# Weight-stationary products with both parts of the activations in one 512-column matmul, and the halves added in evacuation

## The chip, the cores and the metric

One NeuronCore of a Trainium2 chip runs the kernel. The metric is the device time of one execution in microseconds (us), as a median over runs; lower is better.

## The reference

Two blocks work on 256 tokens of width 1024, all in float32. Block one: a mixer (a stick-breaking attention and a gated recurrence `hgrn2_chunk_scan` side by side, merged by sigmoid gates), then a mixture of 16 experts with two experts per token. Block two: half a feed-forward, a mixer of 16 attention heads (banded, compressed and selected), half a feed-forward. Cut to the lines that make the products in question:

```python
def mixer_sublayer(...):                      # first mixer
    h = rmsnorm(x, ln1_g)
    proj = h @ w_in                           # q, k, v | q, f, i, g | two gates
    ...
    merged = (jax.nn.sigmoid(gate_sb) * (y_sb @ w_branch_sb)
              + jax.nn.sigmoid(gate_hg) * (y_hg @ w_branch_hg))
    return x + merged @ w_out

def swiglu(h, w_in, w_out):                   # the feed-forwards, D_FF = 2816
    gate, up = jnp.split(h @ w_in, 2, axis=-1)
    return (jax.nn.silu(gate) * up) @ w_out
```

## The kernel before, in words

**Two parts.** The weights come from DRAM as 1 MB units (`Stream`, tiles `raw`). Outside of the experts, `split_next` cuts each unit into two parts of a narrower float type (fp32r): ACT copies it to `whi` (L353) and DVE subtracts to get `wlo` (L365). The activations x^T are cut the same way into `hTh` and `hTl` (names in the code: `xh`, `xl`), each [128, 8, 256]: 8 blocks k of 128 inputs by 256 tokens. A product is the sum hi·xh + hi·xl + lo·xh. `unit` asks for the next unit's split before the present unit is multiplied, so the splits run one unit ahead in the in-order queues of ACT and DVE. The pool of 1 MB tiles (`big`) has six slots: the two parts of x^T and two pairs `whi`, `wlo`.

**The weight-stationary form.** `form_a` (L395) takes a [1024, 256] unit (or, for the branch products, [512, 512]) as the stationary operand. For each 128 columns c of it there are three groups of eight or four matmuls of 256 columns of tokens into one half of a PSUM bank `psa`:

```python
for k in range(kt):
    nc.tensor.matmul(ps[:, c % 2], hi[:, k, cs], xh[:, k, :], ...)   # L414
    nc.tensor.matmul(ps[:, c % 2], hi[:, k, cs], xl[:, k, :], ...)   # L415
for k in range(kt):
    nc.tensor.matmul(ps[:, c % 2], lo[:, k, cs], xh[:, k, :], ...)   # L419
```

After two such column blocks `evac` empties the bank. The evacuations are: `scaled` (L691, DVE, times the rows' scale `rb`) for the forget gate `sgf`, the query `qh`, the key `kT` and the two merge gates `gr`; `ev_sq` (L705) for `qT`; `ev_sb` and `ev_hg` for the branch products; and `ev` (L1434) in the feed-forward. The other forms are `form_b` and `out_unit` (L483, L490), where the weights are the moving operand, 512 columns at a time.

**What sets the order.** The first mixer (0 to 212 us) is written as one program with two side streams, the recurrence `hgrn` and the attention `stick`, which are interleaved with the units by an estimate of TensorE's clock (`tick`). Outside of the parts under `manual_schedule` the framework's scheduler puts the instructions of each engine into their order. Then come the experts (to 463 us), the first feed-forward (FFN1, to 655 us), the second mixer (to 784 us), which a list scheduler of the kernel (`Plan`) orders from written costs, and the second feed-forward (FFN2, to 970 us). The feed-forwards run in program order: two "q" units (one bank of 128 columns of gate and of up each) to one "o" unit (`out_unit`), a step later. `ev` of a q unit scales at once; its silu (L318), the product with the up half (L1438) and the split into `ah` (L386) and `al` (L387) are put off behind the next unit's split. At the end of FFN1 `then` adds to x (L1470) and makes y (L1474), `turn` transposes y (L1363), and the last split of that stage runs on POOL.

PSUM has four banks for these products in the first mixer, the experts and FFN1 (tag "d", four more have tag "s"). In the second mixer and FFN2 all eight have one tag; FFN2's sums hold five.

Of the kernel before, what the change touches and what calls it, by code (L numbers as in the profile page):

```python
# [10 lines left out]
F32 = mybir.dt.float32  # L11
# [30 lines left out]
RAW = (U_MIX + 6, U_MIX + 7)   # used as they are  # L42
# [17 lines left out]

def bcast_rows(ap2d, off, n):
# [3 lines left out]
def _order():  # L65
    """unit of each place in the stream: an expert's last two units follow the next one's first four"""
# [6 lines left out]
def _part(raw, k, n, c):  # L73
    """columns of block k of n, in a unit of one or more tiles"""
# [4 lines left out]
class Stream:  # L79
    """The packed weights, 1 MB units in the order of use, through slots in SBUF."""  # L80
# [8 lines left out]
    def add(self, pool, tag, bufs, end=N_UNITS, n=1, parts=1, between=None):  # L89
        """n slots, each of `parts` tiles, in a pool that lives until unit `end` is first needed"""  # L90
# [38 lines left out]
# when the parts of x^T are there, from the start of the second mixer  # L129
# [4 lines left out]
class Plan:  # L134
    """Instructions with what they read and write, put into an order by a list schedule:
    at each engine's next free moment the ready one with the longest way to go."""
# [7 lines left out]
    def hold(self, slot, n, key):  # L144
        """key keeps n of a slot's tiles from the start"""
# [3 lines left out]
    def op(self, eng, ns, fn, r=(), w=(), a=(), get=(), at=0.0, p=0.0, seq=None):  # L149
        """reads r, writes w, adds to a in any order; seq: a sequence to keep to"""  # L150
# [34 lines left out]
    def turn(self, key):  # L185
        """whether an addition to key is the first one, and the last one"""
# [9 lines left out]
    def order(self):  # L196
        """by the longest way to go, with a head start for some parts"""
# [71 lines left out]
class K:  # L269
# [6 lines left out]
    # ---- interleaving of instruction streams by an estimate of the PE's clock  # L276
# [26 lines left out]
    # ---- activation tables, in an order that loads each set once per phase  # L303
# [80 lines left out]

    def split(self, hi, lo, src):
# [3 lines left out]
    # ---- products  # L389
    def form_a(self, n, xs, evac, more=True, kt=8, cols=256, first=False):  # L390
        """[kt*128, cols] units as the stationary operand: out^T per 128 columns."""
        nc = self.nc
        xh, xl = xs
        for u in range(n):
# [3 lines left out]
            if first:  # L398
                ps = self.ps.tile([128, 2, 256], F32, name="psa", tag=self.tag("d"))
                for i, (w, v) in enumerate(((hi, xh), (hi, xl), (lo, xh))):  # L400
                    for k0 in (0, 4):
                        for c in range(2):
                            for k in range(k0, k0 + 4):
                                nc.tensor.matmul(ps[:, c], w[:, k, c * 128:c * 128 + 128], v[:, k, :], start=i + c + k == 0,  # L404
                                                 stop=i == 2 and k == kt - 1, skip_group_check=True)
                self.tick(48 * 109)
                evac(u, ps)
                continue
            for c in range(cols // 128):
# [3 lines left out]
                for k in range(kt):  # L413
                    nc.tensor.matmul(ps[:, c % 2], hi[:, k, cs], xh[:, k, :], start=k == 0, stop=False)  # L414
                    nc.tensor.matmul(ps[:, c % 2], hi[:, k, cs], xl[:, k, :], start=False, stop=False)  # L415
                    if k % 4 == 3:
                        self.tick(870)
                for k in range(kt):
                    nc.tensor.matmul(ps[:, c % 2], lo[:, k, cs], xh[:, k, :], start=False, stop=k == kt - 1)  # L419
# [4 lines left out]
    def form_b(self, xs, evac, ps=None):  # L424
        """two [512, n] units as the moving operand: out rows of tokens; with ps, the first one is done"""
# [1644 lines left out]
T4 = 16  # L2070
# [143 lines left out]
```

## Time and profile before

| | us |
|---|---|
| three runs | 974.76, 975.59, 978.01 |
| median | 975.59 |
| span of the profiled execution, first to last instruction | 973.7 |
| TensorE busy in it | 955.5 |
| VectorE (DVE) busy | 539.5 |
| ScalarE (ACT) busy | 408.1 |
| GpSimd (POOL) busy | 106.6 |

The profiled execution has no time of its own beside its span; the median lies 1.9 us above the span. The profile counts an engine as busy while it executes, PE stands for TensorE's matmuls, and PEclk is the clock that TensorE was granted, as a share of full speed. A matmul's own duration overlaps with the next one's, so the pitch of a row of matmuls (from start to start) is read from the chain of work that ended last or from the gaps between starts, not from the duration of one.

### The profile page before, as it was taken

Reading aid. Unit: us, or ns where it says so; the run is one execution under the profiler, and the core shown is the slowest. Engines: PE = TensorE matmul, PEld = TensorE weight load, DVE = VectorE, ACT = ScalarE, POOL = GpSimd, SP = SyncE. Lnnn points to the kernel's source line nnn. Section 1 sums busy time; section 2 is a strip of 40 time slices with the busy share of each in tenths; the row PEclk is TensorE's granted clock in tenths of the full one; section 3 lists DMA queues with packets and bytes.
Section 4 is the critical chain, followed back from the end, with each engine's and each line's share of the span. In section 5 each row is a group of like instructions: output and inputs, shape, how many; then the busy total and the mean of one; then the engine's idle time right before and its main releaser. Section 6 shows DMA issues by size and latency. Waiting matters only on the chain.

```text
span 973.7 us, 15302 instructions
## 1 busy us (share of the span) xinstructions
PE 955.5 (98%) x6320; PEld 762.2 (78%) x6320; DVE 539.5 (55%) x848; ACT 408.1 (42%) x635; POOL 106.6 (11%) x114
## 2 busy tenths in 40 slices
PE   7999999999999999999899999998999999999998
PEld 5997789997444344443799999997987799999997
DVE  5589937665212121222775655657889575655554
ACT  6436644543121111112644434435748644434432
POOL 4143305021000000021400000012000000000000
PEclk9999999999999999999999999999999999999999
DMA  9833274799999999974655555547452255555511
GB/s 337 340 131 130 94 263 140 251 323 353 384 421 418 416 420 416 420 300 174 240 178 211 174 177 195 192 134 253 167 179 82 87 179 207 178 178 175 199 55 44
DMA packets 39321, 224.32 MB, mean 230 GB/s; under 512 B 4404, under 2 KB 7253, under 8 KB 17360
## 3 DMA queue, kind: packets, MB, share of 16 engines
q1 hardware_dynamic: 38512, 221.57, 61.1%
q0 software_dynamic: 592, 1.61, 0.6%
q8 instruction: 51, 0.84, 0.3%
q14 instruction: 22, 0.18, 0.1%
q10 hardware_dynamic: 144, 0.13, 0.0%
HBM read 222.22 MB, written 1.07 MB: 229 GB/s over the span
## 4 chain that ended last, share of the span: by engine, by line
PE 49%; DVE 1%; ACT 1%; issue 0%; POOL 0%; POOLq 0%; DVEq 0%; ACTq 0%
PE psa L419 8%; PE psa L415 8%; PE psa L414 8%; PE po L483 8%; PE po L490 4%; PE po L1591 2%; PE p L1591 2%; PE qa L1591 1%; PE qb L1591 1%; PE pt L1773 1%; PE po L473 1%; PE psa L404 1%; PE sc L1754 1%; PE pa L1591 1%; DVE y L1474 1%; PE Ob L1780 0%
## 5 line engine op out<-in xcount | busy, mean ns | idle before, releaser
L365 DVE TENSOR_TENSOR wlo<-raw,whi 128x2048 fp32r<-128x2048 f32 (+2 forms) x99 | 217.0, 2197 | 52.4 <-ACT whi L353 50.7
L353 ACT ACTIVATE whi<-raw 128x2048 fp32r<-128x2048 f32 (+2 forms) x101 | 180.4, 1792 | 141.7 <-issue 90.2
L414 PE MATMUL psa<-hTh,whi 128*128 128x256 f32 x928 | 228.6, 284 | 0.0
L415 PE MATMUL psa<-hTl,whi 128*128 128x256 f32 x928 | 227.8, 283 | 0.0
L414 PEld LDWEIGHTS psa<-hTh,whi 128*128 128x128 f32 x928 | 177.9, 192 | 0.9 <-issue 0.5
L415 PEld LDWEIGHTS psa<-hTl,whi 128*128 128x128 f32 x928 | 177.9, 192 | 0.4
L419 PE MATMUL psa<-hTh,wlo 128*128 128x256 f32 x928 | 130.5, 283 | 0.0
L419 PEld LDWEIGHTS psa<-hTh,wlo 128*128 128x128 f32 x928 | 119.9, 192 | 0.2 <-issue 0.2
L1186 PE MATMUL gu<-raw,XT 128*64 128x512 f32 x512 | 115.8, 595 | 0.0
L1186 PEld LDWEIGHTS gu<-raw,XT 128*64 128x64 f32 x512 | 35.3, 137 | 66.3 <-issue 63.4
L1233 DVE SCALAR_TENSOR_TENSOR ds<-dn,ws,ds 64x512 fp32r<-64x512 f32 x32 | 24.0, 750 | 109.1 <-ACT ds L1231 108.6
L1434 DVE TENSOR_TENSOR sg<-psa,rb 128x512 f32<-128x512 f32 x44 | 30.3, 691 | 81.7 <-PE psa L419 77.3
L386 ACT ACTIVATE ah<-sg 128x256 fp32r<-128x256 f32 x44 | 18.4, 418 | 104.4 <-DVE sg L1438 104.4
L1224 PE MATMUL dn<-raw,at 128*64 128x512 f32 x256 | 58.2, 598 | 0.0
L483 PE MATMUL po<-whi,ah 128*128 128x512 f32 (+1 forms) x180 | 50.1, 368 | 0.0
L483 PE MATMUL po<-whi,al 128*128 128x512 f32 (+1 forms) x180 | 49.8, 366 | 0.0
L1231 ACT ACTIVATE ds<-dn,ws 64x512 fp32r<-64x512 f32 x32 | 21.8, 682 | 55.0 <-PE dn L1224 40.6
L1224 PEld LDWEIGHTS dn<-raw,at 128*64 128x64 f32 x256 | 17.0, 136 | 31.5 <-issue 29.5
L490 PE MATMUL po<-wlo,ah 128*128 128x512 f32 (+1 forms) x180 | 40.2, 367 | 0.0
L483 PEld LDWEIGHTS po<-whi,al 128*128 128x128 f32 x180 | 32.4, 188 | 6.1
L490 PEld LDWEIGHTS po<-wlo,ah 128*128 128x128 f32 x180 | 31.7, 188 | 5.8
L1576 DVE TENSOR_TENSOR wlo<-raw,whi 128x1024 fp32r<-128x1024 f32 (+2 forms) x28 | 31.6, 1151 | 8.2 <-ACT whi L1572 8.2
(483 smaller groups left out, 1372.7 us busy)
## 6 DMA issues: line engine op xcount, KB each, us to landing
raw<-W SPq DMA_DIRECT2D x171, 1024.0 KB, 5.9
raw<-W SPq DMA_DIRECT2D x64, 512.0 KB, 9.3
bt<-dr SPq DMA_DIRECT2D x2, 1024.0 KB, 9.0
raw<-W SPq DMA_DIRECT2D x2, 816.0 KB, 4.3
raw<-W SPq DMA_DIRECT2D x2, 768.0 KB, 4.8
gain<-gains POOLq DMA_DIRECT2D x2, 512.0 KB, 6.6
out<-x SPq DMA_DIRECT2D x3, 256.0 KB, 2.0
x<-x SPq DMA_DIRECT2D x2, 256.0 KB, 2.9
```

What stands on the lines that cost most here:

```text
L353: i = self.nc.scalar.activation(hi[:, o], r, AF.Copy).ins
L365: i = eng.tensor_tensor(out=lo[:, o], in0=r, in1=hi[:, o].bitcast(F32), op=OP.subtract).ins
L414: nc.tensor.matmul(ps[:, c % 2], hi[:, k, cs], xh[:, k, :], start=k == 0, stop=False)
L415: nc.tensor.matmul(ps[:, c % 2], hi[:, k, cs], xl[:, k, :], start=False, stop=False)
L419: nc.tensor.matmul(ps[:, c % 2], lo[:, k, cs], xh[:, k, :], start=False, stop=k == kt - 1)
L483: nc.tensor.matmul(p, x[:, ts], hi[:, k, c], start=first and k == 0 and x is xh, stop=False)
L490: nc.tensor.matmul(p, xh[:, ts], lo[:, k, c], start=False, stop=False)
L1186: nc.tensor.matmul(GU[e][i * 64:i * 64 + 64], XT[:, kk, c], w, start=kk == 0, stop=kk == 7)
L1224: nc.tensor.matmul(ps[h % len(ps)][R[h]], AT[e][:, f], _part(raw, k, 2, 1024)[:, h * 512:h * 512 + 512], start=f == 0, stop=f == 3)
L1434: V.tensor_tensor(out=sg, in0=ps, in1=rb[:, None].to_broadcast([128, 2, 256]), op=OP.mult)
L1576: i = V.tensor_tensor(out=two[u][1][:, s], in0=unit(u)[0][0][:, s], in1=two[u][0][:, s].bitcast(F32), op=OP.subtract)
L1591: i = nc.tensor.matmul(out(), l, r, start=first and n == 0, stop=last, skip_group_check=True)
```

## The change

The two parts of x^T lie side by side: `hT0` and `hT1` are [128, 4, 2, 256], four blocks k each, and for each k 256 columns of the high part and 256 of the low. `both(xs, k)` gives the 512 columns of a block; all that writes or reads x^T (`turn`, `form_b`, the start of both mixers) is adapted, and so are the branch inputs `ysb` and `yhg`, whose split comes in two pieces per row block. In `form_a` one matmul of 512 columns per k takes the place of the pair L414, L415. So each c fills a bank of its own, the high half in columns 0 to 255 (to which the eight lo products add) and hi·xl in columns 256 to 511. `evac` is given two banks. `add_halves` brings them together: ACT copies the second halves to SBUF (L394), DVE adds the first halves to them (L396); the scale that was the evacuation is now a DVE operation on SBUF (L707, and L1457 in the feed-forward). `ev_sb` multiplies on POOL instead of DVE. In each feed-forward the q units 0 and 1 keep the narrow form (`wide=i > 1`). The tick per four k goes from 870 to 825.

```diff
+def both(xs, k):
+    per = xs[0].shape[1]
+    return xs[k // per][:, k % per]
...
+    def add_halves(self, d, pss):
+        for c, ps in enumerate(pss):
+            self.nc.scalar.activation(d[:, c], ps[:, 1], AF.Copy)
+        for c, ps in enumerate(pss):
+            self.nc.vector.tensor_tensor(out=d[:, c], in0=ps[:, 0], in1=d[:, c], op=OP.add)
...
-    def form_a(self, n, xs, evac, more=True, kt=8, cols=256, first=False):
+    def form_a(self, n, xs, evac, more=True, kt=8, cols=256, first=False, wide=True):
...
+            if wide:
+                pss = []
+                for c in range(cols // 128):
+                    ps = self.ps.tile([128, 2, 256], F32, name="psa", tag=self.tag("d"))
+                    cs = slice(c * 128, c * 128 + 128)
+                    for k in range(kt):
+                        nc.tensor.matmul(ps, hi[:, k, cs], both(xs, k), start=k == 0, stop=False)
+                        if k % 4 == 3:
+                            self.tick(825)
+                    for k in range(kt):
+                        nc.tensor.matmul(ps[:, 0], lo[:, k, cs], both(xs, k)[:, 0], start=False, stop=k == kt - 1)
+                    self.tick(109 * kt)
+                    pss.append(ps)
+                    if c % 2 == 1:
+                        evac(u * (cols // 256) + c // 2, pss[-2:])
...
             def scaled(d, ps):
-                self.last.append(nc.vector.tensor_tensor(out=d, in0=ps, in1=r2, op=OP.mult).ins.name)
+                self.add_halves(d, ps)
+                self.last.append(nc.vector.tensor_tensor(out=d, in0=d, in1=r2, op=OP.mult).ins.name)
...
             def ev_sb(i, ps):
-                nc.vector.tensor_tensor(out=m1[i // 2][:, i % 2 * 2:i % 2 * 2 + 2], in0=ps, in1=gr[0][:, 2 * i:2 * i + 2], op=OP.mult)
+                m = m1[i // 2][:, i % 2 * 2:i % 2 * 2 + 2]
+                self.add_halves(m, ps)
+                nc.gpsimd.tensor_tensor(out=m, in0=m, in1=gr[0][:, 2 * i:2 * i + 2], op=OP.mult)
...
             def ev(q, ps):
                 sg, ah, al = w[0].rearrange("p (a b) c -> p a b c", a=2)[:, q % 2], w[1][:, q % 4], w[2][:, q % 4]
+                if isinstance(ps, list):
+                    self.add_halves(sg, ps)
+                    ps = sg
                 V.tensor_tensor(out=sg, in0=ps, in1=rb[:, None].to_broadcast([128, 2, 256]), op=OP.mult)
...
-                        self.form_a(1, xs, lambda _, ps: p.append(ps), first=i == 0)
+                        self.form_a(1, xs, lambda _, ps: p.append(ps), first=i == 0, wide=i > 1)
```

The program then has 960 matmuls fewer, and 128 copies L394 and 128 additions L396 more: two of each for 64 evacuations (24 in the first mixer, 20 in each feed-forward).

Three places show what moves. First DVE in the first mixer, around the two units of the query `qh` (the forget gate `sgf` stands before them; `wlo` of `raw_203` is the low part of the unit that is multiplied next). Before:

```order
L691 TENSOR_TENSOR qh<-psa,rb_205 128x512
L365 TENSOR_TENSOR wlo<-raw_182,whi 128x2048
L691 TENSOR_TENSOR qh<-psa,rb_205 128x512
L365 TENSOR_TENSOR wlo<-raw_203,whi 128x2048
L852 MEMSET suf 128x1024
```

And with the change:

```order
L371 TENSOR_TENSOR wlo<-raw_182,whi 128x2048
L396 TENSOR_TENSOR qh<-psa,qh 128x256 x2
L707 TENSOR_TENSOR qh<-qh,rb_205 128x512
L866 TENSOR_SCALAR sgf<-sgf,lb 128x256 x2
L371 TENSOR_TENSOR wlo<-raw_203,whi 128x2048
L396 TENSOR_TENSOR qh<-psa,qh 128x256
L707 TENSOR_TENSOR qh<-qh,rb_205 128x512
L871 MEMSET suf 128x1024
```

The evacuation of the second query unit stood before the split of `raw_203` and now ends behind it.

Second, DVE near the end of the first mixer, at the merge gates `gr` (numbers 260 and 261 are its two tiles); `ho` is the recurrence's output, normed by `hst` and gated by `sgh`. Before:

```order
L691 TENSOR_TENSOR gr_260<-psa,rb_205 128x512
L950 TENSOR_TENSOR ho<-ho,hst 128x1024
L365 TENSOR_TENSOR wlo<-raw_992,whi 128x2048
L953 TENSOR_TENSOR ho<-ho,sgh 128x1024
L691 TENSOR_TENSOR gr_261<-psa,rb_205 128x512
L365 TENSOR_TENSOR wlo<-raw_1076,whi 128x2048
```

And with the change:

```order
L396 TENSOR_TENSOR gr_260<-psa,gr_260 128x256
L371 TENSOR_TENSOR wlo<-raw_904,whi 128x2048
L707 TENSOR_TENSOR gr_260<-gr_260,rb_205 128x512
L396 TENSOR_TENSOR gr_261<-psa,gr_261 128x256
L969 TENSOR_TENSOR ho<-ho,hst 128x1024
L972 TENSOR_TENSOR ho<-ho,sgh 128x1024
L396 TENSOR_TENSOR gr_261<-psa,gr_261 128x256
L371 TENSOR_TENSOR wlo<-raw_988,whi 128x2048
L707 TENSOR_TENSOR gr_261<-gr_261,rb_205 128x512
```

Both operations on `ho` and an addition now stand ahead of a unit's low part, where one of them stood before.

Third, DVE in a feed-forward, around one q unit: `sg` is the unit's scaled output, `ah` and `al` its two parts. Before:

```order
L1434 TENSOR_TENSOR sg<-psa,rb 128x512
L365 TENSOR_TENSOR wlo<-raw_4419,whi 128x2048
L1438 TENSOR_TENSOR sg<-sg 128x256
L387 TENSOR_TENSOR al<-sg,ah 128x256
L1434 TENSOR_TENSOR sg<-psa,rb 128x512
```

And with the change:

```order
L396 TENSOR_TENSOR sg<-psa,sg 128x256 x2
L1457 TENSOR_TENSOR sg<-sg,rb 128x512
L371 TENSOR_TENSOR wlo<-raw_4285,whi 128x2048
L1461 TENSOR_TENSOR sg<-sg 128x256
L400 TENSOR_TENSOR al<-sg,ah 128x256
L396 TENSOR_TENSOR sg<-psa,sg 128x256 x2
L1457 TENSOR_TENSOR sg<-sg,rb 128x512
```

Two additions come in ahead of each scale, and the rest keeps its order.

## Rows read from the trace of the kernel before

**Rows 1.** The page: busy time and share of TensorE with its count of instructions, and the granted clock in 40 slices of the span, in tenths.

```profile
PE 955.5 (98%) x6320; PEld 762.2 (78%) x6320; DVE 539.5 (55%) x848; ACT 408.1 (42%) x635; POOL 106.6 (11%) x114
...
PEclk9999999999999999999999999999999999999999
```

**Rows 2.** The waits of TensorE over the whole span: tile and line that waited, what it waited for, and us in total, times, the longest.

```profile
PE pst L1363 <- DVE y L1474: 2.5, 3, 1.6
...
PE hs L895 <- DVE qz L884: 0.2, 1, 0.2
```

**Rows 3.** Windows of 20 us in the first mixer and one of 25 us in the experts: length, then busy us of PE, weight loads, DVE, ACT and POOL (instructions in brackets), granted clock, share of time that the DMA engines were busy, GB/s.

```profile
60.00:80.00 20.00, 20.00 (x157) 18.93 (x157) 19.00 (x17) 8.28 (x10) 5.63 (x5) 1.00 0.41 150
80.00:100.00 20.00, 19.70 (x108) 15.37 (x107) 17.91 (x21) 13.95 (x23) 4.90 (x4) 1.00 0.31 106
100.00:120.00 20.00, 19.83 (x109) 15.06 (x108) 18.85 (x23) 11.79 (x21) 8.87 (x7) 1.00 0.31 106
160.00:180.00 20.00, 20.00 (x169) 20.00 (x168) 13.76 (x9) 7.48 (x4) 3.48 (x3) 1.00 0.60 211
275.00:300.00 25.00, 25.00 (x134) 11.55 (x132) 5.34 (x11) 5.14 (x11) 0.00 (x0) 1.00 1.02 423
```

**Rows 4.** The instructions of line L414 by tiles: count, then duration in ns (least, median, most), first and last start in us, form.

```profile
L414 PE MATMUL psa<-hTh,whi x928: 274/283/387, 23.2 to 956.8; 128*128 128x256 f32 x186
...
L414 PE MATMUL psa<-ysb,whi x32: 280/283/283, 181.8 to 193.5; 128*128 128x256 f32 x32
...
L414 PE MATMUL psa<-yhg,whi x32: 283/283/385, 195.0 to 205.9; 128*128 128x256 f32 x32
```

**Rows 5.** Pieces of the chain of work that ended last: start, length in us, what. First from FFN1: one pair of hi matmuls, a group of eight lo matmuls of 256 columns, and an o unit of 16 and 8 matmuls of 512 columns. The last two are an o unit of FFN2, where 12 of the 20 and 6 of the 10 matmuls have 512 columns and the rest 256.

```profile
534.25 0.12 PE psa L414
534.37 0.12 PE psa L415
...
539.05 0.96 PE psa L419 x8
540.01 3.65 PE po L483 x16
543.66 1.81 PE po L490 x8
...
815.39 3.75 PE po L483 x20
819.14 1.88 PE po L490 x10
```

**Rows 6.** Groups of like instructions over the span: an ACT copy of 256 columns from PSUM to SBUF, a DVE operation on two operands of 256 columns, and a POOL operation on 512 columns (count, then busy us and mean ns, then idle time before and its releasers).

```profile
L387 DVE TENSOR_TENSOR al<-sg,ah 128x256 fp32r<-128x256 f32 x44 | 18.7, 425 | 21.3 <-ACT ah L386 21.3
L1192 ACT COPY gs<-gu 128x256 f32<-128x256 f32 x32 | 10.4, 376 | 56.5 <-PE gu L1186 56.5
...
L736 POOL TENSOR_TENSOR ml<-m1a,mh 128x512 fp32r<-128x512 f32 x2 | 2.8, 1414 | 4.4 <-ACT mh L735 4.4
```

**Rows 7.** The timeline of ACT, and then that of DVE, over a period of two q units and an o unit in FFN1: start, length in us, instruction, and in brackets the idle time before it with its releaser.

```profile
533.38 1.92 ACT L353 ACTIVATE whi<-raw 128x2048 fp32r<-128x2048 f32 x1 [4.39 <-issue]
...
539.14 1.92 ACT L353 ACTIVATE whi<-raw 128x2048 fp32r<-128x2048 f32 x1 [0.73 <-PE psa L415]
...
550.36 1.92 ACT L353 ACTIVATE whi<-raw 128x2048 fp32r<-128x2048 f32 x1 [4.39 <-issue]
...
534.29 0.69 DVE L1434 TENSOR_TENSOR sg<-psa,rb 128x512 f32<-128x512 f32 x1 [2.98 <-PE psa L419]
535.32 2.29 DVE L365 TENSOR_TENSOR wlo<-raw,whi 128x2048 fp32r<-128x2048 f32 x1 [0.34 <-ACT whi L353]
...
538.44 0.42 DVE L387 TENSOR_TENSOR al<-sg,ah 128x256 fp32r<-128x256 f32 x1 [0.48 <-ACT ah L386]
```

**Rows 8.** The timelines of ACT, POOL, DVE and PE at the end of FFN1.

```profile
651.66 1.90 ACT L353 ACTIVATE whi<-raw 128x2048 fp32r<-128x2048 f32 x1
...
653.64 4.58 POOL L365 TENSOR_TENSOR wlo<-raw,whi 128x2048 fp32r<-128x2048 f32 x1 [172.57 <-ACT whi L353]
...
655.24 3.52 DVE L1474 TENSOR_TENSOR y<-x,gain 128x512 f32<-128x512 f32 x1
...
658.82 0.66 PE L1363 MATMUL pst<-cst,y 128*128 128x128 f32 x4 [1.62 <-DVE y L1474]
```

**Rows 9.** The timelines of DVE, ACT, POOL and PE in the first mixer, around the second query unit.

```profile
46.48 0.69 DVE L691 TENSOR_TENSOR qh<-psa,rb 128x512 f32<-128x512 f32 x1 [2.43 <-PE psa L419]
47.51 2.29 DVE L365 TENSOR_TENSOR wlo<-raw,whi 128x2048 fp32r<-128x2048 f32 x1 [0.35 <-ACT whi L353]
...
47.38 0.61 ACT L318 ACTIVATE sig<-qh 128x512 f32<-128x512 f32 x1
...
48.07 2.89 POOL L702 TENSOR_TENSOR qh<-qh,sig 128x512 f32<-128x512 f32 x1 [2.88 <-ACT sig L318]
...
52.08 2.40 POOL L860 TENSOR_TENSOR kz<-qh,kk 128x1024 f32<-128x1024 f32 x1
...
55.87 1.84 PE L865 MATMUL dgp<-c,kz 128*128 128x2 f32 x16
```

**Rows 10.** The timelines of POOL, DVE and PE in the first mixer, at the merge gates.

```profile
158.54 2.94 POOL L949 TENSOR_TENSOR hst<-hst,mhalf 128x16 f32<-128x16 f32 x1
...
161.51 1.23 DVE L950 TENSOR_TENSOR ho<-ho,hst 128x1024 f32<-128x1024 f32 x1 [1.84 <-POOL hst L949]
162.65 2.28 DVE L365 TENSOR_TENSOR wlo<-raw,whi 128x2048 fp32r<-128x2048 f32 x1
164.86 1.64 DVE L953 TENSOR_TENSOR ho<-ho,sgh 128x1024 f32<-128x1024 f32 x1
...
166.46 1.12 PE L419 MATMUL psa<-hTh,wlo 128*128 128x256 f32 x8
```

More of the change, by code (lines that the diff above doesn't have):

```diff
@@ L413, in form_a @@
                 for k in range(kt):
-                    nc.tensor.matmul(ps[:, c % 2], hi[:, k, cs], xh[:, k, :], start=k == 0, stop=False)
-                    nc.tensor.matmul(ps[:, c % 2], hi[:, k, cs], xl[:, k, :], start=False, stop=False)
+                    for v in range(2):
+                        nc.tensor.matmul(ps[:, c % 2], hi[:, k, cs], both(xs, k)[:, v], start=k + v == 0, stop=False)
                     if k % 4 == 3:
@@ L418, in form_a @@
                 for k in range(kt):
-                    nc.tensor.matmul(ps[:, c % 2], lo[:, k, cs], xh[:, k, :], start=False, stop=k == kt - 1)
+                    nc.tensor.matmul(ps[:, c % 2], lo[:, k, cs], both(xs, k)[:, 0], start=False, stop=k == kt - 1)
                 self.tick(109 * kt)
@@ L438, in form_b @@
                     ts = slice(t * 128, t * 128 + 128)
-                    nc.tensor.matmul(ps[t][:, :n], xh[:, kk, ts], hi[:, k], start=kk == 0, stop=False)
-                    nc.tensor.matmul(ps[t][:, :n], xl[:, kk, ts], hi[:, k], start=False, stop=False)
+                    for v in range(2):
+                        nc.tensor.matmul(ps[t][:, :n], both(xs, kk)[:, v, ts], hi[:, k], start=kk + v == 0, stop=False)
                 self.tick(1.672 * n)
@@ L445, in form_b @@
                     ts = slice(t * 128, t * 128 + 128)
-                    nc.tensor.matmul(ps[t][:, :n], xh[:, kk, ts], lo[:, k], start=False, stop=kk == 7)
+                    nc.tensor.matmul(ps[t][:, :n], both(xs, kk)[:, 0, ts], lo[:, k], start=False, stop=kk == 7)
             self.tick(3.344 * n)
@@ L515, in norm_rows, with two_x @@
         return y
-    def transposed(self, y, hi, lo, f32=None):
-        nc = self.nc
-        for t in range(2):
-            for k4 in range(2):
-                ps = self.ps.tile([128, 4, 128], F32, name="pst", tag="s")
-                for k in range(4):
-                    kk = k4 * 4 + k
-                    nc.tensor.transpose(ps[:, k], y[:, t, kk * 128:kk * 128 + 128], self.ident)
-                dst = (slice(None), slice(k4 * 4, k4 * 4 + 4), slice(t * 128, t * 128 + 128))
-                if f32 is not None:
-                    eng = nc.scalar.copy if (t + k4) % 2 else nc.vector.tensor_copy
-                    eng(f32[dst], ps)
-                else:
-                    self.split(hi[dst], lo[dst], ps)
+    def two_x(self):
+        return [self.big(f"hT{i}", (128, 4, 2, 256)) for i in range(2)]
     def run(self):
@@ L807, in values @@
             if h == 1:
-                self.ysb = [P.tile([128, 4, 256], F32R, name=f"ysb{i}", tag="t4", bufs=T4) for i in range(2)]
+                self.ysb = [P.tile([128, 2, 2, 256], F32R, name=f"ysb{i}", tag="t4", bufs=T4) for i in range(2)]
             if h % 2:
-                self.split(self.ysb[0][:, pt], self.ysb[1][:, pt], OT[pt])
+                self.split(both(self.ysb, pt)[:, 0], both(self.ysb, pt)[:, 1], OT[pt])
         for i in range(10):
@@ L954, in hgrn @@
         self.dbg("yhg_tok", of)
-        self.yhg = [P.tile([128, 4, 256], F32R, name=f"yhg{i}", tag="t4", bufs=T4) for i in range(2)]
+        self.yhg = [P.tile([128, 2, 2, 256], F32R, name=f"yhg{i}", tag="t4", bufs=T4) for i in range(2)]
         for t in range(2):
@@ L960, in hgrn @@
             ts = slice(t * 128, t * 128 + 128)
-            self.split(self.yhg[0][:, :, ts], self.yhg[1][:, :, ts], ps)
+            for i, y in enumerate(self.yhg):
+                self.split(y[:, :, 0, ts], y[:, :, 1, ts], ps[:, 2 * i:2 * i + 2])
     def moe(self, x, po):
@@ L1363, in turn @@
             nc.tensor.transpose(ps[:, k], y[:, t, kk * 128:kk * 128 + 128], self.ident)
-        dst = (slice(None), slice(h * 4, h * 4 + 4), slice(t * 128, t * 128 + 128))
-        i = nc.scalar.activation(xh[dst], ps, AF.Copy)
-        return i, lambda xl: nc.vector.tensor_tensor(out=xl[dst], in0=ps, in1=xh[dst].bitcast(F32), op=OP.subtract)
+        xh, xl = [xs[h][:, :, v, t * 128:t * 128 + 128] for v in range(2)]
+        i = nc.scalar.activation(xh, ps, AF.Copy)
+        return i, lambda: nc.vector.tensor_tensor(out=xl, in0=ps, in1=xh.bitcast(F32), op=OP.subtract)
     def spread_scale(self, r, ps, dg, rb):
@@ L2045, in four @@
                             for k in range(h * 4, h * 4 + 4):
[L2046 removed]
+                                n = nc.tensor.matmul(T[first][:, c], two[15][w][:, k * 256 + c * 128:k * 256 + c * 128 + 128], T[f"x{h}"][:, k - 4 * h, v],
                                                      start=a and k % 4 == 0, stop=z, skip_group_check=True)
@@ L2050, in mixer2 @@
                         pl.op("PE", 428, four, r=[(("xh", "xl")[v], t, h) for t in range(2)] + [(("hi", "lo")[w], 15, h)],
-                              a=[first, (("whi", "wlo")[w], 15)], get=[bank(first, (128, 2, 256))])
+                              a=[first, f"x{h}", (("whi", "wlo")[w], 15)], get=[bank(first, (128, 2, 256))])
             scales(x, f2, "f")
```

70 lines of the change are left out of this document (35 added, 35 removed).

## The prediction

> **What bounds the kernel now.** I read the page's first part first, then the granted clock, the waits of TensorE, the chain of waits, and last the timelines around each place that the change touches. TensorE (PE) is busy for 955.5 us of 973.7 us, and the granted clock reads 9 in every slice [rows 1]: the clock is at its upper level throughout, and there is next to no idle time to win. The waits say the same: apart from the loads at the kernel's start the longest is 1.6 us, at the end of FFN1; in the scan of the first mixer PE waits 0.2 us for DVE [rows 2]. So what counts is how long the matmuls themselves take from start to start, and whether new work on ACT, DVE and POOL makes PE wait where it doesn't now.
>
> The chain gives the pitch. A pair L414, L415 takes 0.12 + 0.12 us, and eight lo matmuls of 256 columns 0.96 us, so 0.120 each. The o unit right behind it has matmuls of 512 columns: 16 in 3.65 us and 8 in 1.81 us [rows 5].
>
> **What is removed.** Hi pairs stand in 928 + 32 + 32 = 992 places [rows 4]; the 32 of unit 1 of the two feed-forwards stay narrow, so 960 become one matmul: 320 in the first mixer (16 units and 4 branch units of 16), 320 in each feed-forward (20 units). No 512-column matmul of `form_a` is in the trace; the nearest rows are the o units, with the same array shape, number type and a whole bank as output: (3.65 + 1.81)/24 = 0.2275 us against 0.240, so 0.0125 us less per pair. From the other side, FFN2's o unit mixes widths: (3.75 - 8 x 0.12)/12 = 0.2325 and (1.88 - 4 x 0.12)/6 = 0.2333, so at worst 0.007 less [rows 5]. I take the purer row: 960 x 0.0125 = **12.0 us gained**, 4.0 in each of three stages; the low end is 6.7 us. At the high end, 8 in 1.81 alone gives 0.2263 and 13.2 us.
>
> [...]
>
> **What is added.** 64 evacuations each get two ACT copies of 256 columns (0.376 us, by L1192) and two DVE additions (0.425 us, by L387) [rows 6]; the scale stays one DVE operation of 512 columns, 0.69 us [rows 7], now from SBUF. That is 48 us of ACT and 54 us of DVE, on engines that are busy 408.1 and 539.5 of 973.7 us [rows 1]. Only where they are late does it cost time.
>
> *Feed-forwards, steady state: 0.* In a period of 16.98 us (533.38 to 550.36) ACT idles 4.39 + 0.73 us before two of its hi splits [rows 7]; the three evacuation parts now cost it 0.75 per q unit, 1.5 per period. The second copy must wait for the end of the unit, about 0.9 us after the hi products end, and stands ahead of the next hi split, which so comes some 1.3 us later. The tightest reader is the o unit: `al` ends at 538.44 + 0.42 = 538.86, and the o unit, which starts at 540.01 (and so asks for it at its second k, 8 x 0.228 = 1.8 us later), now has about 2.8 us in hand; 1.4 remain. DVE idles 2.98 + 0.34 us around one scale and gets 0.85. The banks hold too: each unit takes two instead of one, and the first is emptied while the second is filled. What would be late next is the lo split, which has DVE's 0.85 in front of it and about a unit's length to spare.
>
> *The end of FFN1: +1.3.* The last split's low part runs on POOL, 653.64 + 4.58, behind ACT's hi split of 651.66. DVE's y at 655.24 takes 3.52 us and ends only when POOL has, and PE waits 1.62 us for it [rows 8]. That hi split is late by the same 1.3 us as in every period, POOL with it; it then starts at about 654.9, still ahead of y, and PE waits 1.3 longer. If y came first (a margin of 0.33 us), 2.9 would be won instead, as y itself would take 0.69. Bounds: -2.9 to +1.6.
>
> *The first mixer: +4.2*, in three places.
> - The second query unit: its evacuation ran at 46.48, ahead of the low split at 47.51. Now the second addition stands behind that split: the split ends at 49.80, then addition 0.42, scale 0.69, sigmoid 0.61, so the sigmoid ends at about 51.6 instead of 47.99, 3.6 later. POOL's two products follow it; the second ends at 54.48 today and PE reads it at 55.87 (55.6 with PE's own gain), so 1.1 to 1.4 is covered [rows 9]. That leaves 2.3; but POOL's first product took 2.89 us beside DVE's split and needs 1.41 in a quiet place [rows 6], which gives 1.5 back, and half of that is likely enough. I take +1.4, between 0 and 2.5.
> - The scan, 58 to 121 us: DVE is busy 19.00, 17.91 and 18.85 of each 20 us [rows 3], and six more additions, 2.5 us, go in where only 4.2 of 60 us is idle. If all of it pushes the scan out and PE runs out of units, it is 2.5; if the idle time takes it, 0. I take +1.5.
> - The merge gates: POOL's chain ends at 161.48, DVE's L950 follows, then the low split, ended at 164.93, and PE reads it at 166.46: 1.5 us in hand. L953 (1.64 us) stood behind the split [rows 10]. It now stands ahead of one, with an addition (0.42): 0.56 over. The sigmoid that starts POOL's chain comes after two more copies (0.75). Together +1.3, from 0 to 3.
>
> The experts pass a shift on: they load weights at 423 GB/s with the DMA engines always busy, yet PE is busy 25.00 of 25 us there [rows 3], so PE and not the transfers sets their length.
>
> **The sum.** -12.0 + 1.3 + 4.2 = -6.5 us. The profiled span of 973.7 becomes 967.2; the median lies 1.9 us above the span, so the predicted time is 975.6 - 6.5 = **969.1 us**. A measurement of this kernel can tell about 0.3% from no change, 2.9 us, so faster means under 972.7 and slower over 978.5.
>
> **The rivals.**
> - *All the additions are hidden.* The scan's idle time takes them, POOL's products get quicker, and PE gains 12.0 to 12.5 us: about 963.3 (less, if y overtakes POOL). For it: ACT is under half busy, and DVE has 12 to 14 of 20 us outside of the scan. Against: DVE is full just in the scan. 0.12.
> - *Half is eaten.* Either a pair saves 0.007, as FFN2's rows say: 975.6 - 6.7 + 1.3 + 4.2 = 974.4; or the mixer's waits come to twice my figure: 975.6 - 12.0 + 1.3 + 8.4 = 973.3. Both lie within the bounds of the terms. 0.21.
> - *DVE becomes the bound of the first mixer.* The first mixer has 24 evacuations, 48 additions; those of the first four units come before the scan, which leaves 40, 40 x 0.425 = 17.0 us. If all stood on the path, through the scan and the gates behind it: 975.6 - 12.0 + 1.3 + 17.0 = 981.9. It decides as soon as the mixer's waits exceed 12.0 - 1.3 + 2.9 = 13.6 us. For it: DVE's 19 of 20 us between 60 and 120. Against: the additions of the gates fall where DVE has 13.76 of 20 us [rows 3], and today PE hardly waits for DVE at all. 0.06.
> - *The width buys nothing*: a 512-column matmul from `form_a` costs twice 0.120, because the two parts are read from one tile or because the o unit's pitch has another reason. Then only the waits are left, 975.6 + 5.5 = 981.1. Against it: the o units run the same form at 0.2275. 0.03.
>
> **How the numbers follow.** My forecast, 969.1 us with the mixer's waits between 2 and 7 us (966.5 to 972), has 0.58. Faster is this and the first rival, 0.70; the second is within 0.3%, 0.21; the last two are slower, 0.09. The range reaches from the first rival, 963.0, to the upper edge of the second, 976.5, and leaves out some 0.15.
>
> **What would show it.** In the profile after: 960 matmuls fewer; a pitch of 0.226 to 0.228 us for the wide ones; 20 wide q units of each feed-forward shorter by 0.2 us each, with no new wait; PE's wait for y at the end of FFN1 near 2.9 us; and in the first mixer new waits of PE of about 4 us, at the recurrence's first matmuls, in the scan and at the gates' low parts. It is wrong if the pitch is 0.233 or more, if the feed-forwards show waits for `al` or a low part, or if the first mixer's waits add up to over 8 us.

## The result, and the profile after

The changed kernel takes 980.89 us (median of 5 runs, 979.52 to 984.09), the kernel before 975.91 us in the same session: a ratio of 1.0051, 95% interval 1.0033 to 1.0070. It is slower by half a per cent where 969.1 was forecast, and outside of the range. The profiled execution of after took 982.01 us, 1.1 over the median; its span is 980.2 us against 973.7.

The page of after, answering to [rows 1]: busy times and the granted clock, and below them the instruction fetches of the first queue.

```profile
PE 952.0 (97%) x5360; PEld 717.9 (73%) x5360; DVE 583.7 (60%) x974; ACT 446.9 (46%) x765; POOL 114.7 (12%) x118
...
PEclk9999999999999999999899999999999999999999
...
q8 instruction: 44, 0.72, 0.3%
```

TensorE has 960 matmuls fewer, yet its busy time fell by only 3.5 us, and the clock's row has an 8. TensorE's waits in after, answering to [rows 2]:

```profile
PE pst L1383 <- PEq L1290: 5.2, 1, 5.2
...
PE pst L1383 <- DVE y L1497: 3.5, 2, 2.8
PE psa L432 <- DVE wlo L371: 2.4, 1, 2.4
...
PE dgp L884 <- POOL kz L879: 1.4, 1, 1.4
...
PE hs L914 <- DVE acc L920: 0.6, 1, 0.6
```

Four waits of more than 1 us are new or longer: one of 5.2 us for TensorE's own sequencer behind the experts, the one for y at the end of FFN1, one for a low split at the merge gates, and one at the recurrence's first matmuls `dgp`. Behind each of them the clock fell in this execution. The windows of 2 us after them (the granted clock is the third figure from the end):

```profile
60.00:62.00 2.00, 2.00 (x9) 1.72 (x10) 1.96 (x4) 0.96 (x2) 0.48 (x2) 0.64 0.02 8
62.00:64.00 2.00, 2.00 (x10) 1.90 (x10) 2.00 (x2) 1.62 (x1) 2.00 (x1) 0.50 0.00 0
64.00:66.00 2.00, 2.00 (x11) 1.65 (x10) 1.96 (x4) 0.56 (x2) 0.20 (x1) 1.00 0.80 233
...
180.00:182.00 2.00, 2.00 (x10) 1.80 (x9) 2.00 (x3) 0.38 (x1) 0.00 (x0) 0.51 0.63 188
182.00:184.00 2.00, 2.00 (x8) 1.58 (x6) 1.89 (x4) 0.00 (x0) 0.00 (x0) 0.64 1.01 377
...
480.00:482.00 2.00, 2.00 (x11) 2.00 (x11) 0.41 (x1) 0.78 (x2) 2.00 (x1) 0.50 0.04 8
482.00:484.00 2.00, 2.00 (x11) 2.00 (x11) 1.63 (x3) 1.49 (x3) 2.00 (x1) 0.54 0.00 0
...
668.00:670.00 2.00, 1.19 (x5) 1.19 (x6) 1.97 (x3) 0.00 (x0) 1.87 (x9) 0.54 0.30 57
670.00:672.00 2.00, 2.00 (x7) 1.48 (x7) 1.38 (x3) 0.60 (x1) 0.39 (x2) 0.61 0.98 410
```

0.50 is the lowest that these windows show, and the clock was back at 1.00 some 3 to 5 us after TensorE had work again (from 58.61, 179.55, 479.84 and 668.81; the windows from 64, 184, 484 and 672 read 1.00). By an estimate from these windows, 2 us times the share of the clock that is missing, a fall costs 2 x (0.36 + 0.50) = 1.7 us at 60 us, 1.7 at 180, 1.9 at 480 and at most 1.7 at 668, where TensorE still stood for 0.8 us of the first window: **some 7 us together**, more than the whole loss.

Where the time went, by the starts of the same matmuls in both traces (us):

| from | to | before | after | difference |
|---|---|---|---|---|
| start | first `form_a` matmul | 23.2 | 25.4 | +2.2 |
| there | first out unit of the first mixer | 183.5 | 189.4 | +5.9 |
| there | last down product of the experts | 256.1 | 256.1 | 0.0 |
| there | first o unit of FFN1 | 26.1 | 30.2 | +4.1 |
| there | first product of the second mixer | 174.3 | 172.9 | -1.4 |
| there | last out product of the second mixer | 114.7 | 114.7 | 0.0 |
| there | last o matmul of FFN2 | 191.2 | 187.9 | -3.3 |
| there | end | 4.6 | 3.6 | -1.0 |

FFN2 shows the width by itself: 3.3 us for 320 pairs, 0.0103 us a pair. A timeline says the same; eight wide matmuls start at 28.23 and the lo matmuls behind them at 30.07, 1.84 us against 1.92 for the 16 narrow ones [rows 5]:

```profile
28.23 2.00 PE L428 MATMUL psa<-hT,whi 128*128 128x512 f32 x8
30.07 1.12 PE L432 MATMUL psa<-hT,wlo 128*128 128x256 f32 x8
```

The 2.2 us at the start are not put down to the change: in the kernels below that first matmul stands anywhere between 23.1 and 25.7 us, and the one at 23.1 has the changed kernel's first mixer.

### The profile page after: what moved, and what is told of

Read it like the earlier page. It is cut to its first block, busy times and chain, and to the rows that moved or that the text cites. A ratio compares the mean times of both kernels' runs of the same rounds, so it can differ in the third digit from the quotient of the medians.

```text
span 980.2 us, 13700 instructions
## 1 busy us (share of the span) xinstructions
PE 952.0 (97%) x5360; PEld 717.9 (73%) x5360; DVE 583.7 (60%) x974; ACT 446.9 (46%) x765; POOL 114.7 (12%) x118
## 4 chain that ended last, share of the span: by engine, by line
PE 48%; DVE 1%; ACT 1%; issue 0%; POOL 0%; POOLq 0%
PE psa L428 15%; PE psa L432 8%; PE po L511 8%; PE po L518 4%; PE po L1614 2%; PE p L1614 2%; PE qa L1614 1%; PE qb L1614 1%; PE po L501 1%; PE pt L1796 1%; PE psa L444 1%; PE sc L1777 1%; PE psa L417 1%; PE pa L1614 1%; DVE y L1497 1%; PE pst L1383 1%
## 5 line engine op out<-in xcount | busy, mean ns | idle before, releaser
L371 DVE TENSOR_TENSOR wlo<-raw,whi 128x2048 fp32r<-128x2048 f32 (+2 forms) x99 | 213.8, 2162 | 79.5 <-ACT whi L359 78.0
L428 PE MATMUL psa<-hT,whi 128*128 128x512 f32 x896 | 227.8, 396 | 0.0
L359 ACT ACTIVATE whi<-raw 128x2048 fp32r<-128x2048 f32 (+2 forms) x101 | 180.6, 1791 | 26.1 <-PE psa L428 14.0
L428 PEld LDWEIGHTS psa<-hT,whi 128*128 128x128 f32 x896 | 163.0, 191 | 29.6 <-issue 0.5
L432 PEld LDWEIGHTS psa<-hT,wlo 128*128 128x128 f32 x896 | 123.4, 192 | 11.6 <-DVE wlo L371 2.8
L432 PE MATMUL psa<-hT,wlo 128*128 128x256 f32 x896 | 126.5, 285 | 2.4 <-DVE wlo L371 2.4
L394 ACT ACTIVATE sg<-psa 128x256 f32<-128x256 f32 x80 | 30.0, 379 | 65.0 <-PE psa L432 64.7
L396 DVE TENSOR_TENSOR sg<-psa,sg 128x256 f32<-128x256 f32 x80 | 31.8, 419 | 31.0 <-ACT sg L394 30.9
L1212 ACT COPY gs<-gu 128x256 f32<-128x256 f32 x32 | 10.4, 376 | 56.8 <-PE gu L1206 56.8
```

Source lines behind the costliest of these rows:

```text
L359: i = self.nc.scalar.activation(hi[:, o], r, AF.Copy).ins
L371: i = eng.tensor_tensor(out=lo[:, o], in0=r, in1=hi[:, o].bitcast(F32), op=OP.subtract).ins
L394: self.nc.scalar.activation(d[:, c], ps[:, 1], AF.Copy)
L396: self.nc.vector.tensor_tensor(out=d[:, c], in0=ps[:, 0], in1=d[:, c], op=OP.add)
L428: nc.tensor.matmul(ps, hi[:, k, cs], both(xs, k), start=k == 0, stop=False)
L432: nc.tensor.matmul(ps[:, 0], lo[:, k, cs], both(xs, k)[:, 0], start=False, stop=k == kt - 1)
```

## The experiments

The theory after the comparison (A in the first expectations): the width gains about 10 us, and it is lost in the first mixer, at the end of FFN1, and at a branch behind the experts, each time by a wait and by the clock's fall behind it. Each run is compared with the kernel before as timed in its own session, whose median goes from 974.61 to 976.34.

**mix_narrow, ffn_narrow, all_narrow: the change by parts.** `form_a` narrow with the old evacuations in the first mixer alone, in the feed-forwards alone, in both. The new tiles of x^T stay in all three.

```diff
-    def form_a(..., first=False, wide=True):        # mix_narrow, all_narrow (and the old evacuations)
+    def form_a(..., first=False, wide=False):
...
-    self.form_a(1, xs, lambda _, ps: p.append(ps), first=i == 0, wide=i > 1)    # ffn_narrow, all_narrow
+    self.form_a(1, xs, lambda _, ps: p.append(ps), first=i == 0, wide=False)
```

> The first mixer in the narrow form with its old evacuations, the feed-forwards wide; x^T in the new tiles throughout. Theory A (the change loses in three places: waits of TensorE and the falls of its clock behind them in the first mixer, +9.3 us there; a branch of 5.6 us instead of 0.45 behind the experts, because TensorE's instruction stream is 640 instructions shorter by then; and the end of FFN1): the first mixer is as before, the branch is 0.45 us again, the feed-forwards keep -6.8, the end of FFN1 +2.1: about 971. Theory B (the new tiles of x^T cost 2.2 us at the start and elsewhere, whatever the form): about 973 to 975. Theory C (the branch does not hang on the length of the stream): branch 5.6 us, about 975.

> The feed-forwards in the narrow form, the first mixer wide. Theory A: the first mixer +5.9 as in the changed kernel, the branch 5.6 us (the stream up to it is that of the changed kernel, +4 with the clock's fall), the end of FFN1 as before (1.6 us wait): 984 to 986. Theory B, start included: 986 to 988. Theory C (branch not tied to the stream's length before it): 980 to 982.

> Everything narrow with the old evacuations; only the tiles of x^T and of the branch inputs are new. Theory A: as before, 975.9 within 1 us, branch 0.45 us. Theory B: 978, with the start 2 us later.

Measured: 974.14 (0.9988, 0.9977 to 0.9998), 984.81 (1.0096, 1.0080 to 1.0112) and 978.82 (1.0041, 1.0026 to 1.0057), with before at 974.61. The second is as expected. The other two are misses of theory A. mix_narrow lies 3 us over its 971 (theory B had 973 to 975): its first mixer still has a wait of 2.32 us at the gates. all_narrow, with no wide matmul at all, loses 4.2 us, near theory B's 978, although it starts 0.8 us later than before and not 2. Its trace shows the gates' wait too, with DVE's timeline and then TensorE's:

```profile
167.12 1.23 DVE L965 TENSOR_TENSOR ho<-ho,hst 128x1024 f32<-128x1024 f32 x1 [3.76 <-POOL hst L964]
168.26 2.28 DVE L371 TENSOR_TENSOR wlo<-raw,whi 128x2048 fp32r<-128x2048 f32 x1
...
170.60 1.23 PE L448 MATMUL psa<-hT,wlo 128*128 128x256 f32 x4 [2.32 <-DVE wlo L371]
```

DVE stands 3.76 us, waiting for POOL's `hst`; behind it in the queue is the low split that TensorE needs; TensorE waits 2.32 us and its clock falls (0.63 and 0.52 in the next two windows). In before the same wait for `hst` was 1.84 us and left the split in time [rows 10]. In before the sigmoid `sgh` on ACT and the square of `ho` on DVE, with which the work up to `hst` starts, ran at 148.32 and 148.07, two gate scales ahead of the product of `ho` and `hst`. In all_narrow they ran at 155.75 and 158.09, one gate scale ahead of it, although `ho` was written by 135.7 and DVE stood idle for 2.48 us before that scale. So this loss is not the width's, nor the added work's: the scheduler, given the new tiles, put the start of that work a unit later, while a dependency in the kernel holds the product to its place. Why it chose so is not shown. The branch, too, goes with the wide mixer and not with the wide feed-forwards: 0.45 us in mix_narrow and all_narrow, 5.96 in ffn_narrow.

The fall behind a wait does not always come. mix_narrow has the gates' wait and the same wait of 2.83 us for y as after, and its clock stayed at 1.00 behind both:

```profile
170.75 1.22 PE L448 MATMUL psa<-hT,wlo 128*128 128x256 f32 x8 [2.32 <-DVE wlo L371]
...
662.96 0.66 PE L1379 MATMUL pst<-cst,y 128*128 128x128 f32 x4 [2.83 <-DVE y L1493]
...
172.00:174.00 2.00, 2.00 (x19) 2.00 (x19) 2.00 (x3) 0.07 (x1) 0.00 (x0) 1.00 0.72 283
174.00:176.00 2.00, 2.00 (x19) 2.00 (x18) 1.78 (x3) 1.84 (x1) 0.00 (x0) 1.00 0.42 176
...
664.00:666.00 2.00, 1.83 (x12) 1.37 (x11) 1.97 (x4) 0.83 (x2) 0.54 (x2) 1.00 0.87 348
666.00:668.00 2.00, 1.33 (x10) 1.01 (x9) 1.97 (x4) 1.04 (x3) 0.20 (x1) 1.00 0.98 335
```

In the traces of all the kernels with these waits, the clock fell behind the gates' wait (2.3 to 2.4 us) in 4 of 8, behind the one for y (2.8) in 5 of 7, and behind the one at `dgp` (1.3 or 1.4) in 5 of 6. So the length of a wait alone does not decide it; what does was not tested.

**narrow_gates_later and gates_later: that order undone.** One edit, to all_narrow and to the changed kernel:

```diff
-        self.queue(i, self.last[-5])
+        self.queue(i, self.last[-4])     # ho times hst: one gate unit later
```

> Everything narrow, only the tiles of x^T and of the branch inputs new, and the recurrence's last products queued one gate unit later. Theory A (what the new tiles cost, 978.8 against 974.6, is the order that the scheduler chose, by which DVE waits for POOL ahead of a low split): back to 975, no wait for the low split. Rival (the tiles themselves are slower to read or write): 978 to 979.

> The changed kernel with one edit: the product of the recurrence's output with its norm (DVE, L969) is queued behind the scale of the next gate unit but one place later, so that DVE no longer stands waiting for POOL's chain ahead of a low split that TensorE needs. Theory A (that wait of 2.4 us in the first mixer and the fall of TensorE's clock behind it, 1.7 us, come from this order): 980.9 - 4.1 = 976.8, no wait of the lo matmuls for a low split, clock 1.00 between 176 and 190 us. Rival (PE waits there for something else, or the wait moves to the branch products): 980 to 981.

Measured: 975.61 beside 976.34 (0.9997, 0.9988 to 1.0006), and 977.09 (1.0020, 1.0010 to 1.0029, before 974.77). Both as expected: the tiles themselves cost nothing, and neither trace has a wait of TensorE at the gates. In gates_later the stretch from the first `form_a` matmul to the first out unit takes 185.2 us against 189.4 in after, 4.2 less where 4.1 was expected; beside before of the same session the kernel's loss goes from 5.0 to 2.3 us. The windows of gates_later there:

```profile
178.00:180.00 2.00, 2.00 (x15) 1.79 (x14) 2.00 (x3) 1.25 (x1) 1.30 (x1) 1.00 0.00 0
180.00:182.00 2.00, 2.00 (x13) 1.75 (x12) 1.66 (x3) 0.94 (x2) 0.00 (x0) 1.00 0.98 283
```

**two_banks: the width alone.**

```diff
-                        nc.tensor.matmul(ps, hi[:, k, cs], both(xs, k), start=k == 0, stop=False)
+                        for v in range(2):
+                            nc.tensor.matmul(ps[:, v], hi[:, k, cs], both(xs, k)[:, v], start=k + v == 0, stop=False, ...)
```

> The changed kernel with two matmuls of 256 columns into the two halves of each bank in place of the one of 512: same evacuations, same sums, so the difference to the changed kernel is the width alone. Theory A (0.0106 us a pair): 980.9 + 10.2 = 991, 1 to 3 less where the slower TensorE waits less or where the branch is back at 0.45. Rival (the width buys nothing in this form): 980 to 981.

Measured: 985.16 (1.0104, 1.0086 to 1.0121), 4.3 us over the changed kernel (5.6 when each is taken against before of its own session), where 988 to 991 was expected. Its branch takes 0.45 us again, which hides about 5 us of the difference, and of the four falls of the clock its trace has only the one at 668, which hides about 5 more. Stage by stage it is plainer: its FFN2 takes 191.3 us, before 191.2, after 187.9. So in FFN2 the additions and copies cost nothing and the width is worth 3.4 us. The 16 narrow matmuls of two_banks take 820.71 to 822.63, 1.92 us:

```profile
820.71 2.08 PE L429 MATMUL psa<-hT,whi 128*128 128x256 f32 x16
822.63 1.12 PE L433 MATMUL psa<-hT,wlo 128*128 128x256 f32 x8
```

**pad64, before_pad64, pad64_four: the branch.** Behind the experts stands a branch (L1290 of after, L1270 of before) over code that this input does not need. The pads add 64 small matmuls to the start, where TensorE waits for its first loads:

```diff
+                pz, pp = self.mhalf.bitcast(BF), self.ps.tile([32, 32], F32, name="pp", tag="s")
+                for _ in range(64):
+                    nc.tensor.matmul(pp, pz, pz, start=True, stop=True)      # pad64_four: to four tiles in turn
```

> The changed kernel with 64 small matmuls (32 x 32, on a constant tile, result unused) at the very start, where TensorE waits for its first loads: 128 instructions more in its stream ahead of the branch behind the experts. [...] Theory A (what the branch costs hangs on where its target falls in the blocks in which TensorE's instructions are fetched): branch 0.45 us instead of 5.6, with the clock's fall behind it gone: 980.9 - 5.2 - 1 = 974.7. Rival (the branch is slow because of what the wide form does around it, or because there is less code ahead): branch 5.6 us, 981.

> [...] Theory A (the branch's cost hangs on where it falls in the fetched blocks): the branch takes about 5 us instead of 0.45 and the clock falls behind it: 974.8 + 5 = 979.5 to 981. Rival (the branch of the changed kernel was slow for another reason): 0.45 us, 974.8 within 1 us.

> As pad64 (64 small matmuls at the start of the changed kernel), but written to four banks in turn instead of one, so that the banks that later stages take in turn are those of the changed kernel. pad64 brought the branch to 0.45 us as expected, yet took 978.8 instead of 974.7, with a new wait of 1.7 us for x^T at the end of the first feed-forward. Theory A (that wait is the pad's own: one bank more out of a ring of four shifts which bank the transposes there must wait for): the wait of 1.7 us is gone, branch 0.45 us, 975 to 976. Rival (the branch's gain is paid back in that place whatever the banks): 978 to 979.

The branch on TensorE's sequencer, by its line, in the traces of before, after, pad64 and before_pad64 (ns: least, median, most):

```profile
L1270 PEldq COMPARE_BRANCH  x1: 450/450/450, 465.8 to 465.8; - x1
```

```profile
L1290 PEldq COMPARE_BRANCH  x1: 5622/5622/5622, 473.9 to 473.9; - x1
```

```profile
L1293 PEldq COMPARE_BRANCH  x1: 447/447/447, 470.9 to 470.9; - x1
```

```profile
L1273 PEldq COMPARE_BRANCH  x1: 5621/5621/5621, 467.0 to 467.0; - x1
```

The same branch costs 0.45 or 5.6 us, and 64 matmuls 470 us ahead of it flip it either way. The first instruction queue moved 44 pieces with 0.72 MB in after (its row stands above) and 51 with 0.84 MB in before; two_banks, with the 6320 matmuls of before and the copies and additions of after, moved 51 as well, and mix_narrow, with 5680 matmuls, 46 with 0.75 MB, so the count goes with TensorE's instructions. The 960 matmuls and their weight loads are 1920 instructions less for 0.12 MB, some 62 bytes each; a piece of 16.4 KB so holds about 260 of them by this estimate, and the pad's 128 are half a piece. All sixteen traces sort by the count of matmuls and weight loads ahead of the branch: with as many as in before or 512 fewer (pad64, pad64_four, best, best_four) it takes 0.36 to 0.45 us, with 640 fewer (after, ffn_narrow, gates_later, y_dve), 576 fewer (q_narrow) or 128 more (before_pad64) 4.9 to 6.0. That it hangs on the stream's length is so shown; why it does is not: the place of the target, of which theory A speaks, was not seen.

The times: before_pad64 984.48 (1.0085, 1.0072 to 1.0098, before 976.34), 8.1 us slower for work that changes nothing and 3.5 over the 981 expected at most; of the 8.1, 4.3 lie between the experts and the first o unit. pad64 took 978.78 instead of 974.7, with a new wait of 1.7 us for x^T behind FFN1, which before_pad64 has as well. In pad64_four it is gone: 0.6 us is left in its place, so the one bank more out of a ring of four had shifted which bank the transposes wait for. Yet pad64_four took 979.31 (976.40 to 983.03) instead of 975 to 976, a miss: the branch is at 0.36 us, but a wait of 1.9 us follows it for which the profile shows no cause, and the timed runs scatter by 6.6 us in step with their mean granted clock, 0.997 in one of the two quickest and 0.991 in the slowest. Between the profiled executions the pad is worth 4.3 us (975.9 against 980.2), by the medians 1.6; which falls come in which execution stays open.

**q_narrow and y_dve: the other two waits.** The query units narrow with their old evacuation; the last low split of FFN1 on DVE.

```diff
-            self.form_a(2, xs, ev_q)
+            self.form_a(2, xs, ev_q, wide=False)          # q_narrow, with the old scale in ev_q
...
-                    self.split_next(True)(nc.gpsimd)
+                    self.split_next(True)(nc.vector)      # y_dve
```

> The changed kernel with the two query units of the first mixer in the narrow form and with their old evacuation. Theory A (the wait of 1.35 us for kz at the recurrence's first matmuls comes from the second query unit's evacuation, and it lowers the clock for some 4 us): wait below 0.3 us, clock 1.00 at 60 to 64 us, 32 pairs less wide (+0.3): 980.9 - 1.3 - 1.8 + 0.3 = 978.1. Rival (the scan takes the time back): 980 to 981, with more wait between 60 and 125 us.

> The changed kernel with the last low split of the first feed-forward on DVE instead of POOL. Theory A (y waits for POOL's split, which the added copies and additions have made 1.3 us later; a wait of 2.8 us then lowers TensorE's clock): the wait for y falls to about 1.2 us, no fall of the clock at 668 us: 980.9 - 1.6 - 1.6 = 977.7. Rival (the split on DVE delays y as much as it did on POOL): 980 to 981.

Measured: 975.88 (0.9995, 0.9976 to 1.0014, before 974.77) and 979.89 (1.0043, 1.0028 to 1.0057). In q_narrow the wait at `dgp` and the fall behind it are gone, and the trace has the first mixer 4.4 us shorter, for an expected 2.8: the wait at the gates is still there (2.4 us), but the fall behind it, 1.7 us, did not come in this execution; its runs lie in two groups, 970 to 972 and 975.5 to 979, and the profiled one is of the second, with a branch of 5.2 us. Whether the first group met the short branch is open. In y_dve the longest wait for y is 1.3 us and the clock stays at 1.00 from 664 to 672, and the stretch from the first o unit to the second mixer is 2.3 us shorter than in after (170.6 against 172.9); the median moved by 1.0 only, to 979.89 where 977.7 was expected: the shorter wait and stage are shown, a gain in the timed runs is not. In the profiled execution the fall at `dgp` lasted twice as long as in after, and the timed runs spread from 976.11 to 980.97.

**best, mixn_best, best_four: the repairs together.** best is the changed kernel with the gates' order, the narrow query units, y_dve and a pad of 32; best_four writes the pad to four banks; mixn_best has the whole first mixer narrow, the gates' order and y_dve, and needs no pad.

> The changed kernel with four edits together: the two query units narrow, the recurrence's last products queued one gate unit later, the last low split of the first feed-forward on DVE, and 32 small matmuls at the start (the narrow query units bring 64 instructions back, so 64 more bring TensorE's stream ahead of the branch to 512 fewer than before). Theory A (the gain of the width stands everywhere, and these four places held all that was lost): 980.9 - 4 (gates) - 3 (query) - 2 (y) - 6 (branch and clock) = 966. Rival (the waits move on, above all in the scan, where DVE is full): 970 to 973.

> The first mixer narrow, the feed-forwards wide, the recurrence's last products queued one gate unit later and the last low split of the first feed-forward on DVE. Theory A: the kernel with the narrow mixer took 974.1; without its wait at the gates and the clock's fall behind it (-4) and with an earlier y (-2): 968. Whether this is over or under the run with the wide mixer says what the width is worth in the first mixer once its new waits are gone (theory A: 2 us less for the wide one). Rival (the gates' wait is not what the narrow mixer with the new tiles lost): 972.

> As best, with its 32 small matmuls written to four banks in turn. Theory A: the new wait of 1.7 us and what follows it in the second mixer (3 us together) are gone: 967; and since the first mixer is 2 us shorter than in mixn_best (969.0), 967 is also what that difference gives. Rival: 970, as best.

Measured: best 970.00 (0.9935, 0.9924 to 0.9947) and mixn_best 969.02 (0.9925, 0.9912 to 0.9938), both beside 976.34; best_four 968.69 (0.9925, 0.9909 to 0.9942) beside 975.69. All three beat the kernel before by 6 to 7 us, and the changed one by 11 to 12. The expectations were 1 to 4 us too hopeful, and best stands at its rival's 970. In the first mixer the wide form now pays: 182.3 us in best and best_four against 184.3 in mixn_best, 2.0 us for 288 pairs. But best_four gives 1.7 us of that back in the second mixer (116.3 against 114.6), where its clock fell at 662 us (0.50 and 0.69 in two windows) with no wait for y above 1.3 us, and mixn_best is as quick without a pad. Its waits between 100 and 700 us, the longest:

```profile
PE pst L1379 <- DVE y L1493: 2.2, 3, 1.3
PE psa L417 <- issue: 0.8, 1, 0.8
PE pst L1379 <- DVE y L1438: 0.7, 1, 0.7
```

None is above 1.3 us, and its mean granted clock is 0.999.

## Why the prediction was wrong

**The gain, 12.0 us: right in kind, a fifth too large.** A pair saves 0.0103 us, not 0.0125, so 960 x 0.0103 = 9.9; the low end of 0.007 held it. The pitch came out at 0.230, between the two rows that bounded it, and over the 0.226 to 0.228 that was to be seen.

**The feed-forwards' steady state, 0: right.** FFN2 with the added copies and additions and narrow matmuls took 191.3 us beside 191.2.

**The end of FFN1, +1.3: the wait right, its price not.** POOL's split stood just ahead of y as said (663.66 and 664.03), and TensorE's longest wait grew from 1.62 to 2.83 us [rows 8], by 1.2. y itself took 4.73 us:

```profile
663.66 4.55 POOL L371 TENSOR_TENSOR wlo<-raw,whi 128x2048 fp32r<-128x2048 f32 x1 [168.39 <-ACT whi L359]
...
664.03 4.73 DVE L1497 TENSOR_TENSOR y<-x,gain 128x512 f32<-128x512 f32 x1
```

What was left out is the fall of the clock behind it in after, up to 1.7 us more.

**The first mixer, +4.2: the waits right, the same thing left out.** At `dgp` 1.4 was said and 1.35 came, in part by luck: POOL's product for the second query unit, 2.89 us in before, took 1.29, so all of what it could give back came back and not half. At the gates 1.3 was said, 2.38 came, within its bound of 3. In the scan 1.5 was said, and the waits grew by about 1.0. That is 4.7 us. Two falls of the clock added 3.4; together 8.1 of the 9.2 us that the stage lost before its share of the gain (5.9 + 3.3). The rest has no row. That the gates' wait came from the order was seen in the prediction, but its reason, the second operation on `ho` and an addition ahead of the split, is not the one that all_narrow shows: there that operation stands behind the split as in before, and the wait comes all the same, from the late `hst`. So the cause of that order was the new tiles and not the width.

**What no step of the sum held: the branch**, +3.2 us of waiting (5.21 against 0.39 and 1.58 in two places before) and a fall of 1.9; the table has +4.1 for the stretch, so 1.0 of it came back where no row shows it. The prediction called the experts' stage one that passes a shift on, which it did (256.1 in both); the branch stands behind it.

So the step that failed is in the first paragraph: "the clock is at its upper level throughout, and there is next to no idle time to win" was read as a property of the kernel, and the sum has no term for the clock and none for the branch. In before the two longest waits behind the start, 1.62 us at the end of FFN1 and 1.58 at its start, left the clock at 1.00; in after it fell behind all four long waits, for some 7 us, and the branch took 3.2 more. Between the profiled executions this gives -9.9 + 1.2 + 4.7 + 7.0 + 3.2, with 2.2 at the start and -1.0 at the end 7.4, for a measured 6.5. None of the signs of being wrong that the prediction named came: the pitch was 0.230, the feed-forwards had no wait for `al` or a low part, and the first mixer's waits were 4.7 us. The two rivals that ended slower, at 981.9 and 981.1, had the time almost right for wrong reasons: DVE did not become the bound of the first mixer, and a wide matmul does not cost twice 0.120.

With the four places repaired the kernel takes 968.7 to 970.0 us. That this is near 969.1 is luck: the forecast had 12.0 us of gain and 5.5 of waits, most of which the repaired kernels don't have. From 975.6 the measured gain alone would give 965.7, and the repaired kernels stay 3 to 4 us over it, the query units narrow in two and the whole mixer in the third.

## What to carry to other kernels

Price each new wait of TensorE with and without a fall of the clock behind it: here a wait of 1.35 us cost 3.1 us with its fall, and one of 2.4 us 4.1, so a change that saves 10 us of matmuls can lose it in four waits. The same waits also came without the fall, so one trace does not give the price. Before a change is blamed or praised, run it with its core undone and the rest kept: here the new tiles alone cost 4.2 us through the scheduler's order, and one queue edit gave it back. And after any change of the number of instructions, look at the time of the branches behind it.

## What the runs showed of the hardware

- TensorE's branch behind the experts cost 0.36 to 0.45 us or 4.9 to 6.0 us in the sixteen traces; 64 matmuls more at the start, and nothing else, took it from 0.45 to 5.62 (before and before_pad64).
- The granted clock fell to 0.50 in after behind waits of 1.35 us (with 1.95 us of two-column matmuls right after), 2.38, 2.83 and 5.21 us, and came back some 3 to 5 us after work did. Waits of 2.32 and 2.83 us in mix_narrow and of 1.62 and 1.58 in before left it at 1.00.
- DVE's y on two SBUF operands took 4.73 us in after while POOL's split ran beside it, and ended 0.55 us after it (668.76 and 668.21); two of the same form right behind it took 0.69 each (669.39 and 670.72).
